# Interleaving the loads and matmuls of three small experts with those of five large ones

## The chip, the cores and the metric

The kernel runs on one core of a Trainium2 chip. The metric is the device time of one execution in microseconds (us). Before the change the median of three executions is 3051.67 us (3046.82 to 3052.34). TensorE (PE in the profile) does the matmuls, VectorE (DVE) and ScalarE (ACT) the elementwise work, GpSimd (POOL) some DMAs and gathers, and the queue of SyncE (SP) issues the weight loads.

## The reference, cut to what matters

Two transformer blocks for 256 tokens of width 1024, all in float32. The first block has two layers; the second of them ends in a mixture of experts: each token goes to two of eight experts, and each expert is a gated two-stage product with weights of its own, 3 x 1024 x 3584 floats.

```python
def _moe(x, w_router, w1, w3, w2):
    logits = (xt @ w_router).astype(jnp.float32)
    top_v, top_e = lax.top_k(logits, TOP_K)          # 2 of 8 experts per token
    gates = jax.nn.softmax(top_v, axis=-1)
    ...                                              # tokens sorted by expert, blocks of 128
    def run(args):
        xb, e = args
        return _swiglu(xb, w1[e], w3[e], w2[e])      # (silu(x @ w1) * (x @ w3)) @ w2
    ...
    y = jnp.zeros((T, D), x.dtype).at[stok].add(yb[dest] * sg[:, None].astype(x.dtype))
```

The second block (two hybrid layers with feed-forward, gating, windowed attention and retention) follows on the result.

## The kernel before

All weights flow through one stream. `Stream.load` (L285) issues a DMA of 1 MB into one of four buffers called raw (`RAW_BUFS`), on SP's queue; a load waits until the buffer that it takes, the one used four loads earlier, is free. For the fp32r products `Stream.need` (L321) then splits each half of a raw buffer (a unit: two k-rows of 128 x 512) into a high part wh (a cast on ACT, L338) and the rest wl (a subtraction on DVE, L339); there are six buffers of each. When the second unit of a raw buffer is split, the buffer is free and the next load is issued. `Thread.gemm` (L375) takes a unit with six matmuls: per k-row high x high, high x low, low x high (L390 to L392).

The experts are ranked by how many tokens they got, which is known only at run time; each load therefore reads the number of its expert from a register of SP (L303). The five largest (rank below `BIG`) run as `expert128` with up to 128 slots through the split units: 42 loads of 1 MB each. The three smallest run as `expert64` with up to 64 slots. Their stationary operand has 64 columns, and `gemm_pair` (L396) multiplies raw float32 weights, w1 on one half of the array's columns and w3 on the other (L407). A load of theirs is two DMAs of 512 KB into one raw buffer, 42 such loads per expert; the buffer is free when its four matmuls are done on TensorE.

The experts run one after another in the order 0, 5, 1, 6, 2, 7, 3, 4 (`ORDER`, L51), so a small one stands alone between two large ones; within that order the framework places the instructions of each engine by its own priorities. While the first expert waits for the router, up to 24 extra loads of 512 KB are put into spare activation buffers (raws, L294). The gathers of the tokens of the next expert (`gather`, `gather64`) run as a side job, stepped by the stream's units. `overflow` (L1669) holds a branch, not taken here, for experts with more slots than that; it stands before the first expert, and every engine reads the largest count and branches there (L1684). After the last expert the layer norm follows (L1044, L1060) and two threads of the second block share every weight unit.

Of the kernel before, what the change touches and what calls it, by code (L numbers as in the profile page):

```python
# [18 lines left out]
P = 128  # L19
D = 1024  # L20
# [9 lines left out]
SM_N = 2  # L30
SM_END = 7
TOA = 3
TOB = 3
SMALL_AT = 1
# [8 lines left out]
GATHER_WAIT = 4  # L43
# [7 lines left out]
ORDER = (0, 5, 1, 6, 2, 7, 3, 4)  # L51
# [85 lines left out]
def weight_plan():  # L137
# [3 lines left out]
    def add(key, name, idx, c0, c1, small=0):  # L141
        out.append((key, name, idx, c0, c1, small))
# [8 lines left out]
    for i in range(2):  # L151
# [22 lines left out]
        else:  # L174
            for e in range(8):
                for ci in range(7):
                    small = [SM_N if SMALL_AT <= 7 * e + ci < SM_END else 0 for j in range(2)]
                    add((e, "e1", ci), "expert_w1", (0, e), ci * 512, ci * 512 + 512, small[0])
                    add((e, "e3", ci), "expert_w3", (0, e), ci * 512, ci * 512 + 512, small[1])
                full((e, "e2"), "expert_w2", (0, e), D)  # L180
# [26 lines left out]
def weight_groups(shapes):  # L207
# [5 lines left out]
    for key, name, idx, c0, c1, small in weight_plan():  # L213
# [9 lines left out]
        out.append((key, name, idx, c0, n, kc, small, g))  # L223
# [3 lines left out]
def packed_weights(h):  # L227
# [3 lines left out]
    for key, name, idx, c0, n, kc, small, groups in plan:  # L231
# [4 lines left out]
    return packs  # L236


class Stream:


    def __init__(self, m):
# [7 lines left out]
        self.owed = 0  # L250
        self.pin = True
# [3 lines left out]
    def add(self, key, name, n, kc, small, groups, rank=None):  # L255
        per = part_rows(n)
        lst = []
        for at, k, rows in groups:
            lk = per if len(lst) < small else rows
            for j in range(0, rows, lk):  # L260
                li = len(self.loads)
                self.loads.append(([(name, at, rows, j, lk, n)], lk < rows, rank))
                kk = 0
                while kk < lk:
                    sk = min(per, lk - kk)
                    lst.append(len(self.splits))
                    self.splits.append((li, kk, sk, k + j + kk, n, kc, kk + sk == lk))
                    kk += sk
        assert key not in self.index
        self.index[key] = lst  # L270

    def add_pair(self, key, chunks, kc, rank):

        lst = []
        for g in range(len(chunks[0][2])):
            k, rows = chunks[0][2][g][1:]
            for j in range(0, rows, 2):
                li = len(self.loads)
                self.loads.append(([(name, gr[g][0], rows, j, 2, n) for name, n, gr in chunks], False, rank))
                lst.append(len(self.splits))  # L280
                self.splits.append((li, None, 2, k + j, 512, kc, True))
        assert key not in self.index
        self.index[key] = lst

    def load(self, parts=1):  # L285
        while self.next_load < len(self.loads):
            li = self.next_load
            pieces, small, rank = self.loads[li]
            if rank is not None and rank not in self.m.expert:
                self.owed += 1  # L290
                return
            self.next_load += 1
            if small:
                r = self.m.A([P, 1024], F32, name="raws")  # L294
            else:
                r = self.m.praw.tile([P, 2048], F32, name="raw", tag="raw")
            for i, (name, at, rows, j0, lk, n) in enumerate(pieces):
                v = r[:, i * lk * n:(i + 1) * lk * n].rearrange("p (k n) -> p k n", k=lk)
                if rank is None:
# [9 lines left out]
            if not small:  # L309
                return  # L310
# [10 lines left out]
    def need(self, idx):  # L321
# [1782 lines left out]
```

## Time and profile before

| what | value |
|---|---|
| median of three executions | 3051.67 us |
| the profiled execution | 3051.97 us, its span 3050.2 us |
| TensorE busy / VectorE / ScalarE | 97% / 64% / 50% of the span |
| first to last expert on TensorE | 772.70 to 1744.9 us |
| share of the chain that is waiting for expert weights | 8% of the span |

A busy TensorE is not TensorE at its peak: the profile models a matmul's end and shows 390 ns for one that follows the last after 227 ns, so short waits are hidden in its busy time. What a stretch costs is read from start to start.

### The profile page before, as it was taken

Reading aid. Unit: us, or ns where it says so; the run is one execution under the profiler, and the core shown is the slowest. Engines: PE = TensorE matmul, PEld = TensorE weight load, DVE = VectorE, ACT = ScalarE, POOL = GpSimd, SP = SyncE. Lnnn points to the kernel's source line nnn. Section 1 sums busy time; section 2 is a strip of 40 time slices with the busy share of each in tenths; the row PEclk is TensorE's granted clock in tenths of the full one; section 3 lists DMA queues with packets and bytes.
Section 4 is the critical chain, followed back from the end, with each engine's and each line's share of the span. In section 5 each row is a group of like instructions: output and inputs, shape, how many; then the busy total and the mean of one; then the engine's idle time right before and its main releaser. Section 6 shows DMA issues by size and latency. Waiting matters only on the chain.

```text
span 3050.2 us, 38360 instructions
## 1 busy us (share of the span) xinstructions
PE 2954.7 (97%) x14208; PEld 2273.5 (75%) x14208; DVE 1958.3 (64%) x3240; ACT 1536.7 (50%) x2162; POOL 30.7 (1%) x47
## 2 busy tenths in 40 slices
PE   8999999999899998998999899999999999999998
PEld 6888887888762672572477778888888888888887
DVE  6877555777860771581488965757865655668655
ACT  4665444664750651470377644564454444654543
POOL 0000000000000000000000000000000000000000
PEclk9999999999999999999999999999999999999999
DMA  6445554443989999999999955545555555555553
GB/s 226 152 160 193 183 179 174 165 156 114 377 330 398 365 342 388 377 346 376 384 341 353 362 188 179 196 160 186 177 186 185 185 188 193 171 174 184 180 182 108
DMA packets 124769, 721.53 MB, mean 237 GB/s; under 512 B 14168, under 2 KB 14432, under 8 KB 59168
## 3 DMA queue, kind: packets, MB, share of 16 engines
q1 hardware_dynamic: 120096, 703.54, 63.8%
q0 software_dynamic: 4480, 15.48, 1.5%
q8 instruction: 113, 1.85, 0.2%
q14 instruction: 80, 0.66, 0.1%
HBM read 716.87 MB, written 2.10 MB: 236 GB/s over the span
## 4 chain that ended last, share of the span: by engine, by line
PE 61%; DMA 9%; DVE 3%; issue 1%; ACT 1%; SPq 0%; ACTq 0%; POOLq 0%; DVEq 0%
PE mm L391 18%; PE mm L392 18%; PE mm L390 18%; DMA raw<-in_expert_w_dram 8%; PE mm L407 3%; PE tp L594 2%; DVE wl L339 2%; DMA rows<-xrows,toki 1%; ACT wh L338 1%; PE tp L621 0%; PE rop L2017 0%; SPq L307 0%; PE ps L1854 0%; DVE z L1576 0%; PE pops L1022 0%
## 5 line engine op out<-in xcount | busy, mean ns | idle before, releaser
L339 DVE TENSOR_TENSOR wl<-raw,wh 128x1024 fp32r<-128x1024 f32 (+1 forms) x1064 | 1272.3, 1215 | 613.2 <-ACT wh L338 608.8
L338 ACT CAST wh<-raw 128x1024 fp32r<-128x1024 f32 (+1 forms) x1064 | 1088.3, 1046 | 771.2 <-PE mm L392 679.3
L390 PE MATMUL mm<-wh,tg 128*128 128x512 f32 (+2 forms) x2928 | 1142.3, 390 | 0.3 <-ACT tg L600 0.2
L391 PE MATMUL mm<-wl,tg 128*128 128x512 f32 (+2 forms) x2928 | 1120.9, 383 | 2.4 <-DVE wl L339 2.2
L392 PE MATMUL mm<-wh,tg 128*128 128x512 f32 (+2 forms) x2928 | 1122.2, 384 | 0.0
L392 PEld LDWEIGHTS mm<-wh,tg 128*128 128x128 f32 x2928 | 552.0, 189 | 109.1 <-DVE tg L604 1.2
L391 PEld LDWEIGHTS mm<-wl,tg 128*128 128x128 f32 x2928 | 553.2, 189 | 106.5 <-DVE wl L339 7.4
L390 PEld LDWEIGHTS mm<-wh,tg 128*128 128x128 f32 x2928 | 552.7, 189 | 102.3 <-issue 1.7
L390 PE MATMUL mm<-wh,xe 128*128 128x512 f32 x560 | 223.5, 399 | 10.1 <-DVEq L1684 10.1
L391 PE MATMUL mm<-wl,xe 128*128 128x512 f32 x560 | 224.1, 400 | 8.1 <-DVE wl L339 7.7
L392 PE MATMUL mm<-wh,xe 128*128 128x512 f32 x560 | 220.5, 394 | 0.0
L407 PE MATMUL mm<-raw,xs 128*64 128x512 f32 x672 | 187.6, 605 | 15.4 <-DMA raw<-in_expert_w_dram 14.3
L407 PEld LDWEIGHTS mm<-raw,xs 128*64 128x64 f32 x672 | 52.5, 136 | 136.2 <-DMA raw<-in_expert_w_dram 69.1
L391 PEld LDWEIGHTS mm<-wl,xe 128*128 128x128 f32 x560 | 106.1, 190 | 43.2 <-DVE wl L339 22.1
L390 PEld LDWEIGHTS mm<-wh,xe 128*128 128x128 f32 x560 | 106.1, 190 | 32.3 <-issue 10.5
L392 PEld LDWEIGHTS mm<-wh,xe 128*128 128x128 f32 x560 | 105.9, 189 | 21.0
L1639 DVE TENSOR_TENSOR h<-sl,mm 64x512 f32<-64x512 f32 x21 | 14.5, 691 | 165.4 <-ACT sl L1638 165.4
L600 ACT CAST tg<-tp 128x512 fp32r<-128x512 f32 (+1 forms) x127 | 64.4, 515 | 108.9 <-PE tp L594 108.3
L407 PE MATMUL mm<-raw,hT 128*64 128x512 f32 x336 | 101.0, 609 | 7.5 <-DMA raw<-in_expert_w_dram 6.9
L1638 ACT ACTIVATE sl<-mm 64x512 f32<-64x512 f32 x21 | 12.4, 588 | 179.7 <-PE mm L407 179.7
L601 DVE TENSOR_TENSOR tg<-tp,tg 128x512 fp32r<-128x512 f32 (+1 forms) x127 | 75.4, 600 | 23.3 <-ACT tg L600 21.2
L407 PEld LDWEIGHTS mm<-raw,hT 128*64 128x64 f32 x336 | 27.6, 135 | 78.2 <-DMA raw<-in_expert_w_dram 49.7
(394 smaller groups left out, 1940.3 us busy)
## 6 DMA issues: line engine op xcount, KB each, us to landing
raw<-in_expert_w_dram SPq DMA_DIRECT2D x198, 1024.0 KB, 6.9
raw<-in_expert_w_dram SPq DMA_DIRECT2D x252, 512.0 KB, 7.6
raw<-in_w_in_dram SPq DMA_DIRECT2D x101, 1024.0 KB, 4.8
raw<-in_ffn_w_in_dram SPq DMA_DIRECT2D x88, 1024.0 KB, 4.9
raw<-in_ffn_w_out_dram SPq DMA_DIRECT2D x40, 1024.0 KB, 4.9
raw<-in_dense_w_dram SPq DMA_DIRECT2D x32, 1024.0 KB, 4.9
raw<-in_w_out_dram SPq DMA_DIRECT2D x16, 1024.0 KB, 5.1
raws<-in_expert_w_dram SPq DMA_DIRECT2D x24, 512.0 KB, 12.9
```

The lines of the kernel that those rows point to most:

```text
L338: i1 = nc.scalar.copy(hv, src)
L339: i2 = nc.vector.tensor_tensor(out=lv, in0=src, in1=hv.bitcast(F32), op=OP.subtract)
L390: nc.tensor.matmul(o, xh, wh[:, j, :], start=(k == 0), stop=False)
L391: nc.tensor.matmul(o, xh, wl[:, j, :], start=False, stop=False)
L392: nc.tensor.matmul(o, xl, wh[:, j, :], start=False, stop=(k == kc - 1))
L407: m.nc.tensor.matmul(ps[c * 64:c * 64 + 64, :n], xT(k), w[:, c, j, :], start=(k == 0), stop=(k == kc - 1))
L594: nc.tensor.transpose(tp[:, j, :], src[:, (k0 + j) * P:(k0 + j + 1) * P], self.ident)
L600: nc.scalar.copy(hi, tp[:, :nk, :])
L601: nc.vector.tensor_tensor(out=lo, in0=tp[:, :nk, :], in1=hi.bitcast(F32), op=OP.subtract)
L1638: nc.scalar.activation(sl[64:P, :], ps[0:64, :], AF.Silu)
L1639: nc.vector.tensor_tensor(out=h[odd * 64:odd * 64 + 64, :], in0=sl[64:P, :], in1=ps[64:P, :], op=OP.mult)
```

## The change

Large and small experts become two generators, `larger` and `smaller`, that `run_merged` steps through one stream. `add_experts` lays out that stream: the 210 loads of the large experts are numbered 0 to 209; the 126 loads of the small ones are put at positions 12, 13.41, 14.83, ... so that the last one stands 20 large loads before the end (`SMALL_FROM`, `SMALL_TO`). In the order of loads a large one stands 2.5 positions earlier than in the order of work (`SPLIT_LEAD`), because it has to be split first. The matmuls of a pair are pinned in program order and take the half that was loaded last first; their sum stands in the pool aux instead of mm. The extra raws loads are gone. A mark `hold` stops the splits after the first unit of the first expert until that expert's tokens are gathered. The overflow branch moves behind the last expert; it reloads the tokens from DRAM and repeats the statistics when it is taken. One transposed one-hot tile instead of two for a small expert, and the one-hot in another pool.

```diff
-ORDER = (0, 5, 1, 6, 2, 7, 3, 4)
+SMALL_FROM = 12
+SMALL_TO = 20
+SPLIT_LEAD = 2.5
-GATHER_WAIT = 4
+GATHER_WAIT = 8
...
+    def add_experts(self, one):
+        big, small = [], []
...
+        step = (len(big) - SMALL_FROM - SMALL_TO) / len(small)
+        work, load = [], []
+        for i, x in enumerate(big):
+            load.append((i - SPLIT_LEAD, x))
+            work += [(i + j / len(x[3]), x, u) for j, u in enumerate(x[3])]
+        for i, x in enumerate(small):
+            load.append((SMALL_FROM + i * step, x))
+            work += [(SMALL_FROM + i * step, x, u) for u in x[3]]
...
+        self.hold = len(self.splits) + 1
...
-            if li not in self.raw:
+            if kk is None:
+                self.next_split += 1
+                continue
+            if li not in self.raw or j == self.hold:
                 return
...
-        ps = m.pmm.tile([P, 512], F32, name="mm", tag="mm")
+        ps = m.aux(name="pair")
...
-                for c in range(2):
-                    m.nc.tensor.matmul(ps[c * 64:c * 64 + 64, :n], xT(k), w[:, c, j, :], start=(k == 0),
-                                       stop=(k == kc - 1))
+                for c in (1, 0):
+                    i = m.nc.tensor.matmul(ps[c * 64:c * 64 + 64, :n], xT(k), w[:, c, j, :], start=(k == 0),
+                                           stop=(k == kc - 1))
+                    m.tc.keep_in_program_order(i)
...
+    def run_merged(self, gens):
+        cur = [next(g, None) for g in gens]
+        while any(c is not None for c in cur):
+            i = min((c, i) for i, c in enumerate(cur) if c is not None)[1]
+            self.stream.need(self.stream.ahead(cur[i], SPLIT_BUFS - 2))
...
     def moe(self):
         self.drain(self.route)
+        self.gathers = {BIG: self.gather_side(BIG)}
+        self.run_merged([self.larger(), self.smaller()])
         self.overflow()
-        for i, r in enumerate(ORDER):
-            nxt = ORDER[i + 1] if i < 7 else None
-            yield from (self.expert128 if r < BIG else self.expert64)(th, r, nxt)
```

Three places in the order of instructions. On SP, the loads before, where a large expert ends and a small one begins (128x2048 is a load of a large expert, two of 128x1024 one of a small expert; after "waits" stands the engine that frees the buffer):

```order
L307 DMA raw_10596<-in_expert_w2_dram 128x2048 [waits DMAHW1_49,DVE_49]
L307 ISA
L307 DMA raw_10622<-in_expert_w2_dram 128x2048 [waits DMAHW2_49,DVE_49]
L307 ISA
L307 DMA raw_10652<-in_expert_w1_dram 128x1024 [waits DMAHW3_49,DVE_49]
L307 ISA
L307 DMA raw_10652<-in_expert_w3_dram 128x1024
L307 ISA
L307 DMA raw_10675<-in_expert_w1_dram 128x1024 [waits DMAHW4_49,DVE_49]
```

On SP, the loads now, soon after the first small one:

```order
L333 DMA raw_7897<-in_expert_w1_dram 128x2048 [waits DMAHW1_49,DVE_49]
L333 ISA
L333 DMA raw_7903<-in_expert_w1_dram 128x2048 [waits DMAHW3_49,DMAHW2_49,PE_49]
L333 ISA
L333 DMA raw_7933<-in_expert_w1_dram 128x1024 [waits DMAHW4_49,DVE_49]
L333 ISA
L333 DMA raw_7933<-in_expert_w3_dram 128x1024
L333 ISA
L333 DMA raw_7940<-in_expert_w3_dram 128x2048 [waits DMAHW6_49,DMAHW5_49,PE_49]
```

Before, 42 loads of one kind follow each other; now the kinds alternate, and a load of one kind waits for a buffer that the other kind frees.

On TensorE, before, where the work of a large expert (mm_10607) meets the first pair of a small one (mm_10757):

```order
L390 MATMUL mm_10607<-wh_10707,tg_10469 128x512 [waits Activation_49]
L407 MATMUL mm_10757<-raw_10652,xs_10302 64x512 [waits DMAHW7_49]
L391 MATMUL mm_10607<-wl_10708,tg_10469 128x512 [waits DVE_49]
L392 MATMUL mm_10607<-wh_10707,tg_10469 128x512
L390 MATMUL mm_10607<-wh_10707,tg_10469 128x512
...
L392 MATMUL mm_10607<-wh_10717,tg_10469 128x512
L407 MATMUL mm_10757<-raw_10652,xs_10302 64x512 [waits DMAHW0_49]
L407 MATMUL mm_10757<-raw_10652,xs_10302 64x512 x2
```

On TensorE, now, in the middle of the stage:

```order
L420 MATMUL mm_8644<-wh_8684,tg_8048 128x512
L437 MATMUL pair_8605<-raw_8632,xs_7844 64x512 [waits DMAHW5_49]
L437 MATMUL pair_8605<-raw_8632,xs_7844 64x512 [waits DMAHW4_49]
L437 MATMUL pair_8605<-raw_8632,xs_7844 64x512 x2
L421 MATMUL mm_8644<-wl_8685,tg_8048 128x512
L422 MATMUL mm_8644<-wh_8684,tg_8048 128x512
L420 MATMUL mm_8644<-wh_8711,tg_8048 128x512 [waits Activation_49]
```

The four matmuls of a pair load now stand together between matmuls of a large expert, in all 126 cases; before, one of a pair could stand alone.

On ACT, before, between the router and the first expert (wh are casts of expert 0's weights, xe the copies of its gathered tokens from the sums gp, pe the work of the layer before):

```order
L1304 ACTIVATE pe_7562<-mm_7317 128x512 [waits PE_49,Activation_49]
L338 CAST wh_7477<-raw_7360 128x1024 [waits DMAHW4_49]
L338 CAST wh_7509<-raw_7360 128x1024
L338 CAST wh_7552<-raw_7362 128x1024 [waits DMAHW5_49]
L338 CAST wh_8226<-raw_7362 128x1024
L1495 CAST xe_7546<-gp_7500 128x512
L1495 CAST xe_7549<-gp_7531 128x512
L1672 TENSOR_LOAD cmax_7475 [waits DVE_49]
```

On ACT, now, at the same place:

```order
L1529 CAST xe_7522<-gp_7486 128x512 [waits PE_49]
L369 CAST wh_7436<-raw_7358 128x1024 [waits DMAHW3_49]
L1529 CAST xe_7525<-gp_7507 128x512 [waits PE_49]
L369 CAST wh_7528<-raw_7358 128x1024
L1335 ACTIVATE pe_7554<-mm_7317 128x512 [waits DVE_49,PE_49]
L369 CAST wh_7534<-raw_7360 128x1024 [waits DMAHW4_49]
```

The copies of the tokens move ahead of all casts but one, and the branch's read of the count is gone from here. Outside the stretch from here to the layer norm after the experts, the order of PE, DVE, ACT and SP is row for row the same.

## Rows read from the trace of the kernel before

**Rows 1.** The page: TensorE's busy time; GB/s of the span's 40 slices.
```profile
PE 2954.7 (97%) x14208; PEld 2273.5 (75%) x14208; DVE 1958.3 (64%) x3240; ACT 1536.7 (50%) x2162; POOL 30.7 (1%) x47
...
GB/s 226 152 160 193 183 179 174 165 156 114 377 330 398 365 342 388 377 346 376 384 341 353 362 188 179 196 160 186 177 186 185 185 188 193 171 174 184 180 182 108
```

**Rows 2.** Experts 0, 5, 1, 6, 3+4: us, PE, PEld, DVE, ACT, POOL, PEclk, DMA, GB/s.
```profile
772.70:894.40 121.70, 121.58 (x544) 99.93 (x544) 104.18 (x103) 90.87 (x98) 1.23 (x1) 0.98 0.93 358
894.40:1004.30 109.90, 100.45 (x367) 29.71 (x366) 9.98 (x18) 8.43 (x16) 1.49 (x2) 1.00 0.99 385
1004.30:1131.50 127.20, 122.16 (x540) 96.91 (x541) 112.84 (x112) 91.50 (x103) 2.60 (x1) 1.00 0.93 349
1131.50:1245.90 114.40, 102.97 (x377) 32.12 (x377) 10.22 (x19) 8.44 (x16) 1.48 (x2) 1.00 1.01 387
...
1489.00:1744.90 255.90, 248.92 (x1094) 197.95 (x1094) 227.43 (x222) 184.05 (x205) 1.81 (x2) 0.99 0.95 354
```

**Rows 3.** What SP's queue waited for, expert 6 alone.
```profile
SPq L307 <- PE mm L407: 61.1, 41, 4.2
```

**Rows 4.** What SP's queue waited for, experts 3 and 4 (1500 to 1735 us).
```profile
SPq L307 <- DVE wl L339: 186.4, 77, 5.6
```

**Rows 5.** Groups by line, experts 3 and 4: splits on VectorE and ScalarE.
```profile
L339 DVE TENSOR_TENSOR wl<-raw,wh 128x1024 fp32r<-128x1024 f32 x162 | 189.0, 1220 | 13.9 <-ACT wh L338 13.8
L338 ACT CAST wh<-raw 128x1024 fp32r<-128x1024 f32 x162 | 159.2, 1050 | 15.2 <-DMA raw<-in_expert_w_dram 13.6 <-PE mm L391 1.3
```

**Rows 6.** DMA issues in the same stretch: count, KB, us to landing.
```profile
raw<-in_expert_w_dram SPq DMA_DIRECT2D x78, 1024.0 KB, 6.9
```

**Rows 7.** Chain of waits inside expert 6: start, us, what.
```profile
1145.27 8.02 DMA raw<-in_expert_w_dram
...
1153.33 1.95 PE mm L407 x6
...
1155.30 0.33 SPq L307
...
1155.83 7.82 DMA raw<-in_expert_w_dram
```

**Rows 8.** A 20 us stretch inside expert 6.
```profile
1180.00:1200.00 20.00, 16.89 (x62) 4.72 (x58) 1.31 (x2) 1.18 (x2) 0.73 (x2) 1.00 1.03 410
```

**Rows 9.** TensorE in order of time, start of expert 5: start, us, what.
```profile
897.94 0.50 PE L1611 MATMUL scp<-y,ohT 128*128 128x512 f32 x1
898.28 0.40 PE L1612 MATMUL scp<-y,ohT 128*128 128x512 f32 x1
898.61 1.94 PE L407 MATMUL mm<-raw,xs 128*64 128x512 f32 x8
900.48 0.50 PE L1611 MATMUL scp<-y,ohT 128*128 128x512 f32 x1
```

**Rows 10.** TensorE inside expert 5 and at the start of expert 6.
```profile
957.67 0.66 PE L621 MATMUL tp<-c,h 128*128 128x128 f32 x4 [0.92 <-DVE h L1639]
...
1131.42 1.07 PE L407 MATMUL mm<-raw,xs 128*64 128x512 f32 x2
```

**Rows 11.** TensorE at the start of expert 0: start, us, what, idle time before.
```profile
772.70 0.76 PE L390 MATMUL mm<-wh,xe 128*128 128x512 f32 x1 [10.05 <-DVEq L1684]
```

**Rows 12.** ScalarE in order of time, between the router and expert 0.
```profile
760.18 2.00 ACT L338 CAST wh<-raw 128x1024 fp32r<-128x1024 f32 x2 [1.87 <-DMA raw<-in_expert_w_dram]
...
767.86 1.99 ACT L338 CAST wh<-raw 128x1024 fp32r<-128x1024 f32 x2 [2.64 <-DMA raw<-in_expert_w_dram]
769.76 1.06 ACT L1495 CAST xe<-gp 128x512 fp32r<-128x512 f32 x2
```

**Rows 13.** TensorE behind the last expert.
```profile
1744.69 0.39 PE L392 MATMUL mm<-wh,tg 128*128 128x512 f32 x1
...
1755.89 0.87 PE L594 MATMUL tp<-c,xln 128*128 128x128 f32 x3 [8.68 <-DVE xln L1060]
```

**Rows 14.** One stretch over all expert loads.
```profile
757.00:1741.00 984.00, 923.84 (x3860) 587.51 (x3859) 595.05 (x613) 491.13 (x563) 13.77 (x13) 0.99 0.96 365
```

More of the change, by code (lines that the diff above doesn't have):

```diff
@@ L212, in weight_groups @@
     end = {}
-    for key, name, idx, c0, c1, small in weight_plan():
+    for key, name, idx, c0, c1 in weight_plan():
         kc = shapes[name][-2] // P
@@ L230, in packed_weights @@
     packs = {n: np.empty(m, h[n].dtype) for n, m in end.items()}
-    for key, name, idx, c0, n, kc, small, groups in plan:
+    for key, name, idx, c0, n, kc, groups in plan:
         w = h[name][idx]
@@ L236, in packed_weights, with chunk_loads, pair_loads @@
     return packs
+def chunk_loads(name, n, kc, groups):
+    out = []
+    per = part_rows(n)
+    for at, k, rows in groups:
+        units = [(kk, min(per, rows - kk), k + kk, n, kc, kk + per >= rows) for kk in range(0, rows, per)]
+        out.append(([(name, at, rows, 0, rows, n)], units))
+    return out
+def pair_loads(chunks):
+    out = []
+    kc = chunks[0][2]
+    for g, (_, k, rows) in enumerate(chunks[0][3]):
+        for j in range(0, rows, 2):
+            out.append(([(name, gr[g][0], rows, j, 2, n) for name, n, _, gr in chunks],
+                        [(None, 2, k + j, 512, kc, True)]))
+    return out
 class Stream:
@@ L250, in __init__ @@
         self.owed = 0
+        self.hold = None
         self.pin = True
@@ L253, in __init__ @@
         self.ready = {}
[L255 to L268, printed above, removed]
-        assert key not in self.index
-        self.index[key] = lst
@@ L272, in add_pair @@
[L272 to L283, printed above, removed]
@@ L285, in load @@
-    def load(self, parts=1):
[L286 to L294, printed above, removed]
-            else:
[L296 to L299, printed above, removed]
-                    src = self.m.I[name][at:at + P * rows * n].rearrange("(p k n) -> p k n", p=P, k=rows)
-                else:
-                    w = self.m.I[name].rearrange("(e q) -> e q", e=8)
-                    src = w[bass.ds(self.m.expert[rank], 1), at:at + P * rows * n].rearrange(
-                        "a (p k n) -> p (a k) n", p=P, k=rows)
-                q = lk // parts
-                for j in range(0, lk, q):
-                    self.m.nc.sync.dma_start(v[:, j:j + q], src[:, j0 + j:j0 + j + q])
-            self.raw[li] = r if len(pieces) > 1 else v
-            if not small:
-                return
@@ L319, in start, with ahead @@
             self.load()
+    def ahead(self, j, n):
+        while n and j + 1 < len(self.splits):
+            j += 1
+            n -= self.splits[j][1] is not None
+        return j
     def need(self, idx):
@@ L350, in free @@
         del self.raw[li]
-        if not self.loads[li][1]:
-            self.load()
+        self.load()
 class Thread:
@@ L1426, in reg @@
                                             max_val=7)
-        reg(ORDER[0])
+        reg(0)
         self.stream.pay()
-        for r in ORDER[1:]:
+        for r in range(BIG, 8):
+            reg(r)
+        for r in range(1, BIG):
             reg(r)
@@ L1459, in routing @@
         yield
-        yield from self.gather(ORDER[0])
+        yield from self.gather(0)
+        self.stream.hold = None
     def onehot(self, s, io, pos, sel):
@@ L1682, in overflow @@
         y = self.st([P, 256], name="oy")
+        rows = [self.A([P, D], F32, name="orows") for _ in range(2)]
         turn = [0]
         with tc.If(cnt > 64):
+            for t in range(2):
+                nc.sync.dma_start(rows[t], self.xrows[t * P:(t + 1) * P, :])
             off = self.sm(8, name="off")
```

145 lines of the change are left out of this document (93 added, 52 removed).

## The prediction

> **What bounds the kernel now.** I read the page first. TensorE is busy for 97% of the span, but slices 11 to 23 of the 40 move 330 to 398 GB/s against 108 to 226 elsewhere [rows 1]: that is the expert stage, the only part that the change touches. Split by expert, it shows two kinds of stretch [rows 2]. A small expert takes 110 to 114 us with VectorE busy for 10 of them; SP's queue waits for the matmuls of the pairs [rows 3], and the chain of waits reads buffer free, 0.33 us on SP, 8 us until the load lands, 1.95 us of matmul, buffer free again [rows 7]. That turn of 10.36 to 10.56 us for each of four buffers is 2.60 us per load, and the DMA engines are full at 410 GB/s [rows 8]. So a small expert is bound by transfers. A large expert takes 127 to 128 us, or 3.05 us per load (42 loads), at only 349 to 354 GB/s; SP waits for the splits on VectorE [rows 4], and VectorE is busy for 227 of 256 us [rows 2]. Each of the four buffers turns in 4 x 3.05 = 12.2 us: 6.9 us until the load lands [rows 6], 5.3 us for the splits and the issue. Expert 0, which had extra loads in reserve, took 121.7 us at a granted clock of 0.98 [rows 2]; the missing 2% at the lower of two levels (1.2 instead of 2.4 GHz) is 2.4 us, so TensorE itself wants (121.7 - 2.4) / 42 = 2.84 us per load. While small experts run, TensorE has slack; while large ones run, the DMA engines have some.
>
> **Part by part: the mixed stretch.** Per small load there stand (210 - 12 - 20) / 126 = 1.413 large loads in the new stream. TensorE's need per such period: 1.413 x 2.84 = 4.01 us, and one pair load. That takes 1.87 us from its start to the next product of the other kind (898.61 to 900.48), and each change of kind lengthens its neighbours: 0.33 us before it and 0.34 behind it, where 0.23 is the pitch [rows 9]; together 1.87 + 0.10 + 0.11 = 2.08 us. The small expert's own transposes and scatters, five groups of 0.66 [rows 10] and eight products of 0.23, are 5.1 us per 42 loads, 0.12 each. Sum 6.21 us. The transfers need 2.413 x 1.0486 MB / 410 GB/s = 6.17 us. VectorE needs 1.413 x 227.4 / 84 + 10 / 42 = 4.06 us. So the floor of a period is 6.21 us, TensorE's and the DMA's together.
>
> The ceiling, if overlap brings nothing: each buffer keeps its present turn, (1.413 x 12.2 + 10.4) / 4 = 6.91 us. There are still only four buffers, and a load of one kind now waits for a buffer that the other kind frees. For the lower end speaks that VectorE falls from 89% to about 62% of a period, so that the 5.3 us behind a landing can shrink towards a cast and two subtractions, 1.05 + 2 x 1.22 [rows 5], with 0.33 for SP: 3.8 us. Against it speaks that two engines would both have to run at 94% or more in step. I take the middle, 6.56 us; the neighbouring ends go into the range. 126 periods are 826.6 us.
>
> A rule speaks against mixing. Rows 9 show that a change between 64-column pairs and full-width products costs 0.10 to 0.11 us. The Trainium skill (TensorEngine Tiling (Array Packing), Key Properties) says that switching the tiling mode drains TensorE. The trace agrees in kind; 252 switches at that price are 26 us, which the 2.08 us hold, and a price of nothing would make the floor 6.00 us.
>
> **Head and tail.** The first 12 and last 20 large loads run without small ones at the present pace of 3.05: 36.6 and 61.0 us. The reserve of raws loads is gone, so expert 0's faster pace is not kept; that costs 12 x 0.21 = 2.5 us, already in the 36.6.
>
> **The start.** TensorE stands idle for 10.05 us before expert 0 [rows 11]. The row names the branch's line on VectorE, but the copies of the gathered tokens come at 769.76 us, behind casts that waited for a load until 767.86 [rows 12]. In the new order those copies stand ahead of all casts but the first, and that one's data landed at 760.18. They could run when the gather's products are done, before TensorE ends its previous work, 10.05 us ahead of 772.70, at 762.65. So expert 0 begins at 762.7 instead of 772.7, with the splits then only just ahead of it. The bounds are no gain (if the second split is late by as much) and 12.4 us (with the slow clock gone as well); I take 10.
>
> **The branch.** It cost nothing of its own at the start: TensorE's first product followed the copies. At the end it stands in a gap of some 11 us, from the last product to the first transpose, in which the layer norm runs on VectorE [rows 13]. It is one read of a count that has long been there and one jump per engine. Behind it wait the layer norm, TensorE's transposes and SP's next weight loads; six loads are issued ahead of it, which cover 1744.9 to 1756. I take 0, bounds 0 and the 10.05 us at which the row at the start would put it. The longer waits of the gathers (8 steps instead of 4) stand beside 42 loads of other work, cost nothing, and would cost one landing, some 8 us, where that cover failed. The fewer copies of the one-hot and the other pool for the sums have the same answer: below 1 us each, either way.
>
> **The sum.** 762.7 + 36.6 + 826.6 + 61.0 = 1686.9 us for the end of the last product, where it is now 1744.9 [rows 13]: 58.0 us earlier. The layer norm and all that follows are the same instructions in the same order. The profiled execution took 3051.97 us, 0.3 us above the median of the three runs: 3051.97 - 58.0 = 2994.0, and I say 2994 us.
>
> **The rivals.**
> - Both floors are met. For it: expert 6 shows that four buffers can keep the DMA engines full [rows 8], and TensorE ran at its pace where loads were in reserve. Against: large experts alone lose 7% against TensorE's pace with transfers at 84%. Period 6.21: 860.3 + 782.5 = 1642.8, 102 us less, 2950 us.
> - The buffers keep their turns. For it: same buffers, same issue, same landing of 7 to 8 us. Against: the part of VectorE that eases. Period 6.91: 1731.0, 14 us less, 3038 us.
> - It gets slower: a pair load that lands early holds its buffer until TensorE comes to it. Before, it was used as soon as it landed; now it stands in one queue behind units of large experts, which need that buffer for their next load, and a load's place in SP's queue cannot be passed. A wait of x us per small load adds x / 4 to the period; from 6.91 it is slower than before when the period passes 7.02, so from about x = 0.45 us. With x = 2 the period is 7.41 and the time 3052 + 49 = 3101 us. For it: large loads are put 2.5 positions ahead so that small ones come late, but the shift is fixed and the pace is not. Against: a stall of TensorE also holds up the splits, which lets the transfers catch up.
> - Transfers go no faster than they do. The stage moves 365 GB/s on average now [rows 14], with peaks of 410. If that average were the limit, the same 352 MB (eight times three matrices of 14.7 MB) would take as long as they do and only the start could move: within 6 us of 3052. The Trainium skill (DMA: Bandwidth & Descriptors, Where 436 GB/s comes from) states that the memory side binds at about 358 GB/s per core, which would make it 352 / 358 = 984 us, no gain. The 410 GB/s held over 20 us contradict it for this run.
>
> **How the numbers follow.** Forecast (period 6.4 to 6.75, 2974 to 3018 us) 44%; floors met (2950 to 2974) 20%; turns kept (3018 to 3045) 19%; transfers limit, no change 6%; slower 11%. The likeliest case gives 2994. The range is 2952 to 3042 us: it leaves out the slow case, the no-change case and the edge of the best. 0.2% (6 us) is what a measurement of this kernel can tell from no change. Faster by more than that 0.83, within 0.06, slower 0.11.
>
> **What would show it.** In the new profile: expert 0's first product at about 762.7 with no idle time before it that the copies explain; the slices of the mixed stretch at 375 to 400 GB/s without the pattern of 350 and 410; a start-to-start distance of pair loads near 6.56 us; pair loads of 1.9 us with neighbours 0.1 us longer; VectorE near 60%; the last product near 1687 us; and a gap before the next block that stays near 11 us. The prediction is wrong if TensorE's pair products wait for loads by more than 1 us each, if SP's waits for them grow, or if the gap at the end grows by the branch.

## The result, and the profile after

The changed kernel takes 3064.55 us (median of 6 runs, 3058.07 to 3071.77), the kernel before 3049.89 us (6 runs, 3046.82 to 3053.19) on the same chip. The ratio is 1.0055, with a 95% interval of 1.0044 to 1.0067: slower by 0.55%, where 2994 us and a range of 2952 to 3042 were forecast. The profiled execution took 3071.77 us, with a span of 3070.0. It is the slowest of the six, 7 us above the median, which is less than 0.06 us in each of the periods below.

The page of the kernel after, the lines of [rows 1]: TensorE's busy time, and GB/s by slice.

```profile
PE 2958.3 (96%) x14208; PEld 2242.6 (73%) x14208; DVE 1960.1 (64%) x3240; ACT 1536.9 (50%) x2161; POOL 27.9 (1%) x47
...
GB/s 225 154 157 192 191 178 162 177 148 134 354 356 349 345 356 362 350 381 366 351 355 357 356 204 177 200 165 191 170 181 186 188 187 189 181 172 176 182 187 110
```

The pattern of 350 and 410 is gone, as foreseen, but what took its place is the lower of the two, not 375 to 400. By stretches of the kernel after (columns as in [rows 2]): the head with large loads alone, the mixed stretch, the tail.

```profile
762.70:800.00 37.30, 36.03 (x159) 27.58 (x158) 33.62 (x38) 30.13 (x37) 1.02 (x1) 1.00 0.96 367
800.00:1705.00 905.00, 831.70 (x3427) 481.81 (x3425) 510.72 (x520) 418.88 (x481) 9.96 (x12) 0.99 0.96 357
1705.00:1765.00 60.00, 57.35 (x253) 44.98 (x251) 52.72 (x54) 39.90 (x43) 0.00 (x0) 1.00 0.92 348
```

In the mixed stretch VectorE is busy for 511 of 905 us, 56%, and TensorE for 92%. Nothing is full, and the transfers run at 357 GB/s, though their engines show a busy share of 0.96.

TensorE in order of time: expert 0's first product, the first pair load, the last product of the experts and the first transpose of the next block (they answer to [rows 11] and [rows 13]).

```profile
762.65 0.39 PE L420 MATMUL mm<-wh,xe 128*128 128x512 f32 x1
...
806.89 1.94 PE L437 MATMUL pair<-raw,xs 128*64 128x512 f32 x8
...
1766.74 0.73 PE L1656 MATMUL scp<-y,ohT 128*128 128x512 f32 x2
1776.38 0.88 PE L635 MATMUL tp<-c,xln 128*128 128x128 f32 x3 [8.91 <-DVE xln L1091]
```

The start and the end are as forecast: no idle time before expert 0, which begins at 762.65, and 8.91 us of waiting for the layer norm, where it was 8.68. What lies between is too long. The products of the 126 pair loads start from 806.89 to 1705.18 us: a period (from one pair load to the next) of 7.19 us, where 6.56 was forecast.

SP's waits from 800 to 1705 us (us in total, times, longest; answers to [rows 3, 4]), and the DMA issues of all expert loads (count, KB, us to landing; answers to [rows 6]), both of the kernel after.

```profile
SPq L333 <- DVE wl L370: 442.8, 174, 5.1
SPq L333 <- PE pair L437: 198.5, 123, 8.1
```

```profile
raw<-in_expert_w_dram SPq DMA_DIRECT2D x210, 1024.0 KB, 7.5
raw<-in_expert_w_dram SPq DMA_DIRECT2D x252, 512.0 KB, 6.5
```

From the times of SP's issues, first half to first half, the buffer of a large load turns in 12.24 us and that of a pair load in 11.45, so the period is (1.413 x 12.24 + 11.45) / 4 = 7.19. (The expectations below take 12.08 and 11.70, with the same sum.) The large loads' turn has not shrunk (11.97 for experts 3 and 4 before). From landing to the free buffer they now take 4.7 us on the mean, where it was 5.2, but they land after 7.6 us, where it was 6.7. The pair loads' turn has grown by about 1 us: TensorE starts on a pair load 9.5 us after its issue on the mean, but both halves have landed after 7.5, so it lies for 2.0 us. In the small experts before, TensorE began on the first half before the second had landed.

What ScalarE and TensorE waited for in the same kernel, 800 to 1660 us (the stretch used for every run below).

```profile
ACT wh L369 <- DMA raw<-in_expert_w_dram: 210.9, 97, 5.5
ACT sl L1685 <- PE pair L437: 87.2, 21, 5.5
ACT hT L665 <- PE tp L662: 53.6, 12, 6.1
...
PE mm L421 <- DVE wl L370: 53.3, 75, 1.5
PE mm L420 <- ACT wh L369: 6.1, 12, 2.0
...
PE pair L437 <- DMA raw<-in_expert_w_dram: 1.1, 3, 0.5
```

The pair loads come early (TensorE waits 1.1 us for them in all), the large ones late (ScalarE waits 211 us for them), and TensorE stands still for splits. One place shows the order on the two engines: ScalarE in order of time, then TensorE.

```profile
1138.09 0.59 ACT L1685 ACTIVATE sl<-pair 64x512 f32<-64x512 f32 x1 [3.88 <-PE pair L437]
1138.70 1.99 ACT L369 CAST wh<-raw 128x1024 fp32r<-128x1024 f32 x2
```

```profile
1135.78 0.40 PE L421 MATMUL mm<-wl,tg 128*128 128x512 f32 x1
1136.10 1.94 PE L437 MATMUL pair<-raw,xs 128*64 128x512 f32 x8
1137.97 0.50 PE L422 MATMUL mm<-wh,tg 128*128 128x512 f32 x1
1138.31 0.40 PE L420 MATMUL mm<-wh,tg 128*128 128x512 f32 x1
...
1141.07 0.50 PE L421 MATMUL mm<-wl,tg 128*128 128x512 f32 x1 [0.77 <-DVE wl L370]
```

ScalarE works its queue in order. It stands 3.88 us before the silu of a pair's sums, and the two casts behind it run only then, though their load landed at 1137.15. TensorE, which had little split weight left, waits for the subtraction that follows them. How little is the same in all 21 cases: when the silu runs, ScalarE has cast only 1.2 units that TensorE has not used, some 1.6 us of work. The code asks for four units ahead. But most of that standing costs nothing, because the data behind it have not landed either: the casts here could have begun 0.93 us sooner, not 3.88. Over the 21 silus that is 10.7 of 87.2 us, over the 12 copies of transposes (hT) 25.9 of 53.6.

The instruction order that comes out of the code has moved TensorE's side: of the 125 distances between pair loads 73 hold two units of large experts and 52 hold four, never one or three. The pairs stand at nearly the same place of a large load each time, behind the fifth of its twelve products in 115 of 126 cases, and on the mean 4.8 units behind the place in the written order (24 units for the first, 2.83 more for each that follows).

### The profile page after: what moved, and what is told of

It is laid out like the page before. It is cut to its first block, busy times and chain, and to the rows that moved or that the text cites. A ratio compares the mean times of both kernels' runs of the same rounds, so it can differ in the third digit from the quotient of the medians.

```text
span 3070.0 us, 38248 instructions
## 1 busy us (share of the span) xinstructions
PE 2958.3 (96%) x14208; PEld 2242.6 (73%) x14208; DVE 1960.1 (64%) x3240; ACT 1536.9 (50%) x2161; POOL 27.9 (1%) x47
## 5 line engine op out<-in xcount | busy, mean ns | idle before, releaser
L370 DVE TENSOR_TENSOR wl<-raw,wh 128x1024 fp32r<-128x1024 f32 (+1 forms) x1088 | 1301.7, 1215 | 763.7 <-ACT wh L369 759.6
L369 ACT CAST wh<-raw 128x1024 fp32r<-128x1024 f32 (+1 forms) x1088 | 1113.7, 1045 | 971.8 <-PE mm L422 664.6
L421 PE MATMUL mm<-wl,tg 128*128 128x512 f32 (+2 forms) x2928 | 1124.4, 384 | 17.8 <-DVE wl L370 17.5
L421 PEld LDWEIGHTS mm<-wl,tg 128*128 128x128 f32 x2928 | 553.2, 189 | 130.7 <-DVE wl L370 30.4
L421 PE MATMUL mm<-wl,xe 128*128 128x512 f32 x560 | 229.2, 409 | 41.2 <-DVE wl L370 40.8
L420 PE MATMUL mm<-wh,xe 128*128 128x512 f32 x560 | 225.0, 402 | 5.3 <-ACT wh L369 5.2
L422 PE MATMUL mm<-wh,xe 128*128 128x512 f32 x560 | 229.1, 409 | 0.0
L421 PEld LDWEIGHTS mm<-wl,xe 128*128 128x128 f32 x560 | 105.7, 189 | 90.9 <-DVE wl L370 66.5
L437 PE MATMUL pair<-raw,xs 128*64 128x512 f32 x672 | 162.7, 605 | 1.1 <-DMA raw<-in_expert_w_dram 0.9
L437 PEld LDWEIGHTS pair<-raw,xs 128*64 128x64 f32 x672 | 40.7, 136 | 79.5 <-issue 75.7
L437 PE MATMUL pair<-raw,hT 128*64 128x512 f32 x336 | 84.2, 623 | 0.2 <-DMA raw<-in_expert_w_dram 0.2
L635 PE MATMUL tp<-c,h 128*128 128x128 f32 x360 | 55.5, 274 | 6.3 <-DVE h L1638 6.3
L635 PEld LDWEIGHTS tp<-c,h 128*128 128x128 f32 x360 | 43.3, 140 | 22.1 <-DVE h L1638 11.1
L651 ACT ACTIVATE tg<-tp,gt 128x128 fp32r<-128x128 f32 x160 | 45.5, 376 | 24.7 <-PE tp L635 24.7
```

The costliest lines, as they stand in the source:

```text
L369: i1 = nc.scalar.copy(hv, src)
L370: i2 = nc.vector.tensor_tensor(out=lv, in0=src, in1=hv.bitcast(F32), op=OP.subtract)
L420: nc.tensor.matmul(o, xh, wh[:, j, :], start=(k == 0), stop=False)
L421: nc.tensor.matmul(o, xh, wl[:, j, :], start=False, stop=False)
L422: nc.tensor.matmul(o, xl, wh[:, j, :], start=False, stop=(k == kc - 1))
L437: i = m.nc.tensor.matmul(ps[c * 64:c * 64 + 64, :n], xT(k), w[:, c, j, :], start=(k == 0), stop=(k == kc - 1))
```

## Experiments

Four theories. A: only the order of the loads is wrong (pair loads too early). B: four buffers are too few, in any order. C: the transfers themselves run no faster than some 360 GB/s when the kinds alternate. D: the order on TensorE and ScalarE is wrong, because the pairs were moved. In the expectations, the wait of 2.2 us is the time that a landed pair load lies. Ratios are to the kernel before, measured beside each.

**One number each: the loads' order, the buffers.** In the changed kernel

```
-SPLIT_LEAD = 2.5
+SPLIT_LEAD = 3.5        (first run; 1.5 in the second)
```
```
-RAW_BUFS = 4            -SLOTS = 23
+RAW_BUFS = 5            +SLOTS = 21      (third run)
```

> The changed kernel with SPLIT_LEAD 3.5 instead of 2.5: each large load is issued one large load earlier against the pair loads, so a pair load comes later in the queue; nothing else differs. Theory A (pair loads come too early, land, and hold one of four buffers for 2.2 us until TensorE reaches them, while the large ones come late): that wait goes, the turn of a pair load falls from 11.7 towards 10 us and the period from 7.19 to about 6.7 us, 126 x 0.5 = 60 us less: about 3000 us. Theory B (four buffers are too few whatever the order: a late pair load only exchanges its wait in the buffer for a wait of TensorE): period within 0.1 us of 7.19, time within 15 us of 3064. Theory C (the transfers themselves run no faster than some 357 GB/s when the two kinds alternate): no change, 3064.

> The changed kernel with SPLIT_LEAD 1.5 instead of 2.5: each large load is issued one large load later against the pair loads. Theory A: pair loads wait longer in their buffers (2.2 us becomes about 5), large loads come later, the period grows by 0.5 to 1 us: 3064 + 63 to 126 = about 3130 to 3190 us. Theory B: the place of a load in the queue matters little, within 20 us of 3064. Theory C: no change as long as the DMA engines have loads to move, 3064.

> The changed kernel with five buffers for weights in place of four (and 21 slots in place of 23 for the activations, to make room). Theory A: the early pair load no longer costs a buffer, period down to about 6.4 us. Theory B: the turns of 12.1 and 11.7 us are shared by five, (1.413 x 12.08 + 11.70) / 5 = 5.75, below the floor of 6.21, so the period is 6.2 to 6.4 us, 100 to 125 us less in the mixed stretch, and the single-kind stretches and other parts of the kernel gain a little too: about 2950 us. Theory C: the rate stays at 357 GB/s, the loads only take longer (7.5 us to landing becomes 9 or more), and the time stays at 3060.

Lead 3.5: 3056.83 us, 1.0032 [1.002, 1.0045]; lead 1.5: 3061.83 us, 1.0048 [1.0031, 1.0064]. Periods 7.08 and 7.13. Neither is what A wanted, but A does not fall by it. Without a pin the order on TensorE moved with the loads: the pairs stand 6.8 units behind their written place at lead 3.5, 4.8 at 2.5 and 2.8 at 1.5. Counted in large loads, those issued ahead of a pair load are 0.6 more than those that TensorE is through with when the pair starts, in all three kernels. The lead shifted both orders together, and what A is about did not change. Five buffers: 3042.68 us, 0.9984 [0.9975, 0.9994], period 6.99. That is a fifth of what B wanted (0.7% or 21 us of more than 100), and TensorE still waits for splits:

```profile
PE mm L421 <- DVE wl L370: 43.6, 56, 1.5
```

**The slots alone**, as a control for every run with five buffers (SLOTS 21, four buffers).

> The changed kernel with 21 slots for activations in place of 23 and nothing else: the control for the runs with five buffers. If the slots have no part in those, within 6 us of the changed kernel, 3064 (ratio to before about 1.004); if fewer slots by themselves cost or bring something, that belongs to every run with five buffers.

3065.98 us, 1.0059 [1.0042, 1.0076]: the slots have no part in it.

**The start alone**, on the kernel before: the hold on expert 0's splits, and the branch behind the experts, as in the change's diff.

```
+            if li not in self.raw or j == self.hold:
...
-        self.overflow()
         self.lnf = ...
         for i, r in enumerate(ORDER): ...
         th.flush()
+        self.overflow()
```

> The kernel before with only two parts of the change: the splits of expert 0 held back until its tokens are gathered, and the branch for further slots moved behind the experts. The experts keep their order one after the other. Expert 0's first product starts at 762.7 instead of 772.7 us, and the gap behind the last expert stays near 11 us: 3052 - 10 = 3042 us. If the start's gain is given back because expert 0 then waits for its splits or loads: 3050. If the branch at the end costs what the row at the start named: 3052.

3047.43 us, 0.9997 [0.9987, 1.0007]: no gain that can be measured, and of the three cases the one at 3050, where the gain is given back. TensorE of this kernel, at the first and last product of expert 0 and at the last pairs of expert 5, and in the kernel before at the last product of expert 0:

```profile
760.32 0.40 PE L391 MATMUL mm<-wh,xe 128*128 128x512 f32 x1
...
887.46 0.39 PE L393 MATMUL mm<-wh,tg 128*128 128x512 f32 x1
...
997.82 1.93 PE L408 MATMUL mm<-raw,hT 128*64 128x512 f32 x6 [0.21 <-DMA raw<-in_expert_w_dram]
```

```profile
894.04 0.39 PE L392 MATMUL mm<-wh,tg 128*128 128x512 f32 x1
```

Expert 0 begins 12.4 us earlier than before (772.70), but its last product comes only 6.6 us earlier, and the last pairs of expert 5, which is bound by transfers, 4.5 us earlier (1002.30 before). So about half of the gain is lost within expert 0, which had its extra loads ready when it began later, and some more in the stretch that waits for transfers. Which wait took it inside expert 0 is not shown.

**The order on TensorE.** The first product of a large expert behind a pair load is pinned behind it; nothing else.

```
 gemm:
-                nc.tensor.matmul(o, xh, wh[:, j, :], start=(k == 0), stop=False)
+                i = nc.tensor.matmul(o, xh, wh[:, j, :], start=(k == 0), stop=False)
+                if m.stream.behind:
+                    m.stream.behind = False
+                    m.tc.keep_in_program_order(i)
 gemm_pair:
                     m.tc.keep_in_program_order(i)
+            m.stream.behind = True
             m.stream.free(li)
```

> The changed kernel with one pin more: the first product of a large expert behind each pair load may not be moved ahead of it on TensorE. In the changed kernel the pair loads stand only where two or four units of the large expert are through (73 and 52 times of 125); here they stand where the written order puts them, after three units in 65 cases, two in 32, four in 20. On ScalarE the copy that waits for a pair's sums then has three to six casts of later units ahead of it on TensorE's count, where it had one. Theory D (TensorE's order was moved: a pair stands up to four units too late, so its load lies in the buffer for 2.2 us, and ScalarE, waiting for that pair's sums, leaves TensorE only one unit, 1.4 us, of split weights): the wait of a landed pair load falls below 1 us, TensorE's waits for splits fall from 55 to below 25 us, the period from 7.19 to about 6.7 us, 3064 - 60 = about 3000 us. Theory A (only the order of the loads counts): pairs come earlier on TensorE, so their loads wait less, as under D, but large loads stay late: period about 7.0, 3040 us. Theory B (four buffers are too few in any order): period 7.1 to 7.2, 3055 to 3064 us, and TensorE waits for pair loads instead.

> The same pin with SPLIT_LEAD 1.5: the pair loads are issued one large load earlier again. If under the pin the pair loads come too late (TensorE waits for them), this takes that wait away, and the time is below that of the pin alone, by up to 30 us; if they come in time there, the pair loads lie in their buffers by some 4 us more and the time is 20 to 60 us above it. Theory B: within 15 us of the pin alone.

> The same pin with five buffers (21 slots for activations). Theory D: with five buffers alone TensorE still waited 46 us for splits while ScalarE waited 123 us for pairs; with the pin as well the stage comes near the floor, period 6.25 to 6.5 us against 6.99 with five buffers alone, 3043 - 60 to 3043 - 95 = 2950 to 2985 us. Theory C (the transfers run no faster than some 365 GB/s on the mean of the stage, whatever the order): within 10 us of 3043.

The pin alone: 3080.4 us, 1.011 [1.0088, 1.0131], slower still, and outside all three theories' numbers. TensorE's waits have changed sides, to the one that B named:

```profile
PE pair L441 <- DMA raw<-in_expert_w_dram: 63.6, 39, 4.5
...
PE mm L425 <- DVE wl L371: 4.2, 6, 0.9
PE mm L421 <- ACT wh L370: 3.6, 4, 1.9
```

TensorE hardly waits for splits any more, as D had said; but the pairs now stand earlier and their loads are late. With the loads' order shifted to fit (lead 1.5) the time is 3044.37 us, 0.9987 [0.9976, 0.9999], 36 us less, a little more than was expected. With five buffers instead it is 2993.47 us, 0.9822 [0.9805, 0.984], period 6.59, a little above the range that D gave. Its stretch from 800 to 1660 us:

```profile
800.00:1660.00 860.00, 830.90 (x3558) 511.16 (x3559) 545.23 (x547) 454.27 (x504) 10.20 (x12) 0.99 1.00 388
```

388 GB/s over 860 us: theory C falls.

**Is it the mixing at all?** The kernel before with the start's edits and five buffers (21 slots), experts one after the other.

> The kernel before (experts one after the other) with five buffers, 21 slots, and the start and the branch of the change. If buffers alone hold the large experts at 3.05 us a load, they come to 2.84 to 2.9, 210 x 0.15 to 0.2 = 30 to 40 us less, about 3010 us, and the interleaving is worth only what lies below that. If VectorE (89% busy there) holds them, within 10 us of 3045.

3036.42 us, 0.9955 [0.994, 0.997]: the second case, VectorE, at the edge of its range. Beside the same kernel with four buffers (0.9997) the buffer is worth 0.4% without mixing; with mixing and the pin it is worth 2.8% at lead 2.5 (1.011 to 0.9822). Interleaving pays once it is fed: with five buffers the ratio is 0.9822 against 0.9955 one after the other.

**Where the loads' order counts.** The pin with both numbers of buffers at other leads, and lead 0.5 without the pin.

> The pin with five buffers and SPLIT_LEAD 1.5, so pair loads are issued one large load earlier. With the pin and five buffers TensorE still waits 9 us for pair loads. If pairs are still late there, that wait goes and the time falls by up to 10 us below 2993; if early pair loads now take a buffer from the large ones again (theory A), TensorE waits for splits and the time lies 5 to 30 us above 2993. Theory B: within 5 us.

> The pin with four buffers and SPLIT_LEAD 0.5. At 2.5 TensorE waited 64 us for pair loads (3080), at 1.5 43 us (3044). If four buffers only want the right order of loads (theory A), the wait falls on and the time comes to 3010 to 3030. If four buffers are too few for both kinds at once (theory B), large loads come late instead and TensorE waits for splits: 3040 to 3075, with the least near 1.5.

> The pin with four buffers and SPLIT_LEAD -0.5: pair loads one large load earlier than in the run at 0.5 (3025 us, period 6.82, TensorE waiting 25 us for splits and 15 us for pairs). If four buffers still only want the right order, the 15 us of waiting for pairs go: 3010 to 3020 us. If the best place is passed (theory B, four buffers too few for both kinds), TensorE's waits for splits grow by more than the pairs' shrink: 3030 to 3060 us.

> The changed kernel with SPLIT_LEAD 0.5 and no pin: the same order of loads as in the run of 3025 us, but on TensorE the pairs stand after two or four units (73 and 52 times) and ScalarE has one unit in reserve behind each of their copies. If the loads' order did it (theory A), 3025 to 3035 us. If the order on TensorE and ScalarE is needed as well (theory D), 3050 to 3065, as at 1.5 and 3.5 without the pin.

> The pin with five buffers and SPLIT_LEAD 0.5. At 1.5 TensorE waits only 3 us for pairs and 15 us for splits, so there is little left: 2985 to 3000 us. If early pairs hold buffers that the large loads miss even with five, 3000 to 3015.

Together, with TensorE's waits for splits (L421 or L425, and the casts) and for pair loads, and GB/s, all from 800 to 1660 us (the period from the first pair load to the last). Everything but the last two columns is from one profiled execution of each kernel, up to 7 us off the median:

| buffers | pin | lead | period us | splits us | pairs us | GB/s | time us | ratio |
|---|---|---|---|---|---|---|---|---|
| 4 | no | 3.5 | 7.08 | 56.4 | 1.8 | 363 | 3056.83 | 1.0032 |
| 4 | no | 2.5 (the change) | 7.19 | 59.4 | 1.1 | 356 | 3064.55 | 1.0055 |
| 4 | no | 1.5 | 7.13 | 57.2 | 2.2 | 360 | 3061.83 | 1.0048 |
| 4 | no | 0.5 | 7.07 | 50.7 | 2.4 | 363 | 3062.26 | 1.0053 |
| 4 | yes | 2.5 | 7.23 | 7.8 | 63.6 | 355 | 3080.40 | 1.0110 |
| 4 | yes | 1.5 | 7.00 | 14.3 | 43.1 | 369 | 3044.37 | 0.9987 |
| 4 | yes | 0.5 | 6.82 | 27.8 | 15.0 | 376 | 3025.07 | 0.9926 |
| 4 | yes | -0.5 | 7.94 | 98.1 | none listed | 323 | 3167.17 | 1.0388 |
| 5 | no | 2.5 | 6.99 | 47.7 | none listed | 366 | 3042.68 | 0.9984 |
| 5 | yes | 2.5 | 6.59 | 7.4 | 8.8 | 388 | 2993.47 | 0.9822 |
| 5 | yes | 1.5 | 6.57 | 15.3 | 3.3 | 390 | 2990.29 | 0.9810 |
| 5 | yes | 0.5 | 6.57 | 19.3 | 0.9 | 389 | 2991.09 | 0.9813 |

Without the pin the time stays within 8 us for leads from 0.5 to 3.5; at 0.5, too, the pairs moved along (0.9 units behind their written place) and the 0.6 of a large load stayed. With the pin the lead shifts one order against the other: at 2.5, 1.5, 0.5 and -0.5 the large loads issued ahead of a pair load are 2.6, 1.7, 0.7 and -0.2 more than those that TensorE is through with. Now the loads' order counts as A had said, 3080, 3044 and 3025 us, until the best place is passed.

The pin itself is seen best at lead 0.5 with four buffers, where SP issues the same loads in the same order with and without it. Without the pin, then with it:

```profile
800.00:1660.00 860.00, 797.95 (x3303) 462.25 (x3301) 488.43 (x500) 403.39 (x463) 10.87 (x12) 1.00 0.97 363
```

```profile
800.00:1660.00 860.00, 810.91 (x3421) 481.21 (x3418) 508.34 (x520) 421.20 (x481) 10.76 (x12) 1.00 0.99 376
```

The pin takes 37 us, 3062.26 to 3025.07, as D had said. TensorE starts on a pair load 8.7 us after its issue instead of 9.5. The pair load's turn falls from 11.46 to 10.68 us, the large one's only from 11.92 to 11.81, so of the 0.23 us that the period loses by these turns the pair load brings 0.20. The fifth buffer brings the next 34 us, 3025.07 to 2991.09: B was right that four are too few, and wrong that the order does not matter.

Whether the pin works through TensorE's order alone or also through ScalarE's is not separated. When the silu of a pair's sums runs, one whole unit stands cast ahead of TensorE without the pin; with it there are mostly five or six at lead 2.5 and three to six at 1.5, but only one or two at 0.5. With five buffers these three take 2993, 2990 and 2991 us, so the number of units in reserve does not decide it there. Nor does ScalarE's standing. Pin, five buffers, lead 0.5:

```profile
ACT sl L1690 <- PE pair L441: 81.3, 21, 6.0
...
ACT hT L670 <- PE tp L667: 38.1, 12, 4.3
...
PE mm L425 <- DVE wl L371: 17.8, 27, 1.3
...
PE mm L421 <- ACT wh L370: 1.5, 8, 0.2
```

ScalarE stands for pairs and transposes nearly as long as in the changed kernel (119 us against 141), and TensorE waits a third as long for splits (19.3 us against 59.4).

Lead -0.5 with four buffers is a cliff, 100 us beyond what B had expected of it. There the rival "a pair load that lands early holds its buffer" is plainest: a landed pair load lies for 6.1 us, and SP's waits turn round (compare 442.8 and 198.5 above):

```profile
SPq L334 <- PE pair L441: 363.0, 106, 5.7
SPq L334 <- DVE wl L371: 231.2, 91, 6.6
```

TensorE's granted clock there is 0.94 over the stretch, against 0.99 to 1.00 in the other runs but two (0.97 and 0.98, four buffers with the pin at 2.5 and 1.5), so part of the 3167 us is time at the lower of its two levels. With five buffers the lead hardly counts between 2.5 and 0.5.

**ScalarE in written order too**, with the pin and five buffers: casts, the silus of both kinds, and the small experts' copies of their sums and transposes, each pinned behind what stands before it on ScalarE (two of the edits shown, the others are alike).

```
-            if j == 0:
+            if j == 0 or self.loads[li][1] is not None:
                 m.tc.keep_in_program_order(i1)
...
+            self.tc.keep_in_program_order(nc.scalar.activation(sl[64:P, :], ps[0:64, :], AF.Silu))
```

> The pin with five buffers, and ScalarE's casts of expert weights and its copies of the small experts' and silu's results kept in written order, so that four units of splits stand ahead of each copy that waits for a pair, where five or six did. If what counts on ScalarE is that TensorE has more than one unit in reserve (theory D), the time stays within 10 us of 2993; if ScalarE now waits in front of data that have not landed while finished sums lie, it is 10 to 40 us above.

3015.7 us, 0.9894 [0.9877, 0.991]: 22 us above the pin alone (2993.47), outside what D allowed. TensorE waits 20.0 us for pairs instead of 8.8. So the written order on ScalarE is no gain. The number is that of the expectation's other case, 10 to 40 us above; that case's reason is not shown. Which of the pinned instructions costs it was not tried.

The version at lead 1.5 with pin and five buffers beats both kernels: 2990.29 us, 0.9810 [0.9793, 0.9827]; its intervals overlap with those of 0.5 and 2.5.

## Why the prediction was wrong

**The start (gain 10, bounds 0 and 12.4): right as a place, wrong as a gain.** Expert 0 began at 762.65, forecast 762.7. On the sequential kernel the same edit brought nothing (0.9997), so the term may have stood for more than it was worth; in the changed kernel it was not measured by itself.

**Head and tail: right only in their sum. Branch: right.** The first pair load came at 806.89, 7.6 us behind 762.7 + 36.6, because it had been moved; with the pin (five buffers, lead 1.5) it comes 37.8 us after expert 0's start instead of 44.2. From the start of the last pair load to the end of the last weight product it was 60.2 us, where one period and 61.0, or 67.6, were forecast. What moved behind large loads at the head was missing at the tail. The branch cost 0.2 us of waiting (8.91 against 8.68).

**The 2.08 us of a pair load: right. The floor of 6.21: not contradicted, but no run reached it.** With the pin and five buffers the period came to 6.57 to 6.59. The pair load's price is in the rows above: 1136.10 to 1137.97 is 1.87 us, with 0.32 us before it and 0.34 behind it where the pitch is 0.23. That two engines run "at 94% or more in step" was held to be unlikely and is possible: at 388 GB/s TensorE is busy for 830.9 of 860 us, 97% by the profile's busy time.

**The period of the mixed stretch: the step that failed.** It read "The ceiling, if overlap brings nothing: each buffer keeps its present turn", 6.91 us, and "I take the middle, 6.56 us". The measured period, 7.19, lies above that ceiling. 125 x (7.19 - 6.56) = 79 us, and the last weight product (1765.3) came 78 us behind the forecast 1686.9. It was no ceiling, for a buffer's turn holds the waits of the engine that empties it, and these depend on what stands ahead in that engine's queue. The pair turn of 10.4 was taken from a stretch where TensorE did nothing but wait for pairs [rows 7]; among large units a landed pair load lies for 2.0 us and the turn became 11.45. The large turn, 12.2, was to shrink because VectorE eased. VectorE did ease (56%, forecast near 60%), and the 5.3 us behind a landing became 4.7, but the landing grew from 6.9 to some 7.5 and the turn stayed at 12.24. In place of the ceiling the runs showed that the order decides: with the pin and the loads' order to fit, the pair turn is 10.68 and the period 6.82, below 6.91, and only the fifth buffer brings 6.57.

The prediction has no row of ScalarE, which was 50% busy and was taken for free. Its queue held 21 silus that wait for pairs and 12 copies that wait for transposes, 141 us of the 860. How much of that cost TensorE anything stays open: by the landings at most 37 us of it held back casts, and in the fast kernel above (pin, five buffers, lead 0.5) 63 of its 119 us did.

**The rival that came true** is the third, at 11%: "a pair load that lands early holds its buffer until TensorE comes to it". The pair turn grew from 10.4 to 11.45, which is 0.26 us of a period, the large one from 12.2 to 12.24, 0.01; added to 6.91 that is 7.18, near the measured 7.19. The sum has to come out, since a period is the turns shared by four buffers; what it tells is where the growth lies. Its price, x / 4, was about twice too high: a pair load lay for 2.0 us and its turn grew by 1.05. Its cause was half right. "The shift is fixed and the pace is not" would make the lead the cure. The lead alone cured nothing, because TensorE's order moved with it; with the pairs pinned, the lead took 55 us (2.5 to 0.5). The order shown ahead of the prediction was read for which instructions stand together, not for how far the pairs stand from their written place and from their loads.

**The rival of the mean rate** (no change) fell with 388 to 390 GB/s over 860 us. The Trainium skill (DMA: Bandwidth & Descriptors, Where 436 GB/s comes from) puts the memory side at about 358 GB/s per core. The changed kernel's 357 looked like that bound; the pin and the fifth buffer, which leave the loads and their order as they are, took the same bytes to 388, and the lead to 390, so it was none here.

The forecast of 2994 us is met within 0.2% by the kernel with the pin and five buffers, 2990 to 2993. That is no success of the number: it was forecast for four buffers, and the best order found with four gives 3025 us and 6.82. Five give 6.57.

## What to carry to other kernels

When two kinds of work are put on one stream, compare for each engine the order that comes out with the order in which the loads are issued, and ask how long a landed load waits for the engine that frees its buffer. A number that shifts both orders together, as the lead did here, tests neither. An engine that stands at the head of its queue costs only as much as the work behind it was ready. A buffer's turn measured in one regime is no bound for another; only the price of the casts and products inside it carried over here, and the landing did not (6.9 us before, 7.5 after). Take order and buffers together: here a better order with four buffers was slower until the loads were moved to fit, and a fifth buffer was worth 0.7% without the pin, 2.8% with it at lead 2.5, and 1.1% at lead 0.5, which suits four buffers best.

## What the runs showed of the hardware

The busy share of the DMA engines is a poor sign of how full they are: 0.96 went with 357 GB/s, 0.99 with 390. A 1 MB load of the same shape lands in 7.5 us at 357 GB/s and, with five buffers and the pin, in 7.7 to 8.8 us at 388 to 390 GB/s. An estimate from the mean times to landing and the periods has 2.5 loads in flight in the first case and 3.0 to 3.2 in the second: the rate still grew with the loads in flight, and the time to landing with it. A pair load once took 3.05 us instead of 1.94 on TensorE, at a mean granted clock of 0.63, so mostly at the lower of its two levels; TensorE had stood 0.41 us for a cast and 1.07 us for a split just before, and up to 1210 us the clock was 1.00 (five buffers, no pin). The row of TensorE and that of the stretch:

```profile
1212.75 3.05 PE L437 MATMUL pair<-raw,xs 128*64 128x512 f32 x8
```

```profile
1212.75:1215.80 3.05, 3.05 (x10) 0.83 (x10) 0.00 (x0) 0.00 (x0) 0.00 (x0) 0.63 0.95 322
```
